# The first projection of a decoder trunk: its loads in halves, products from the first microsecond, small loads later

## The chip, the cores and the metric

One NeuronCore of a Trainium2 chip runs the whole program. The metric is the device time of one execution in microseconds (us); each number below is from one profiled execution or from the three timed runs of the kernel before. The engines are TensorE (PE; its weight loads are PEld), VectorE (DVE), ScalarE (ACT), GpSimd (POOL) and SyncE (SP), which here does nothing but issue DMAs.

## The reference, cut to what matters

One layer: a combined input projection, four token mixers on its columns, gates, an output projection, a LayerNorm, then a mixture of 16 experts and another LayerNorm. x is 256 rows by 1024, float32.

```python
def mixer(x, w_in, ...):
    proj = jnp.einsum("bsd,de->bse", x, w_in)          # 1024 -> 10264 columns
    (a_in, gdn_qkv, ...) = jnp.split(proj, offsets, axis=-1)
    ...
    qkv = jax.nn.silu(causal_depthwise_conv(gdn_qkv, gdn_conv_w))
    ...
    return jnp.einsum("bsd,de->bse", merged, w_out)

def reference(x, ...):
    h = mixer(x, ...)
    x = layer_norm(DN_ALPHA * x + h, ...)
    h = moe(x, ...)
    return layer_norm(DN_ALPHA * x + h, ...)
```

## The kernel before

Every product of the mixer is made in two parts: an operand is split into a rounded high part (`xh`, `whi`, ACT's copy) and the rest (`xl`, `wlo`, DVE's subtraction), and three products (high by high, high by low, low by high) are accumulated in PSUM. `proj_cm` (L277) makes 256 columns of the input projection: two blocks `b` of 128 columns, 8 row blocks `k`, so 2 times 24 products of 128x128 by 256 columns: for a block the 16 with `whi` (L266, L270), then the 8 with `wlo` (L275). Its weights are one 1 MB load (`fetch`, L109) into one of three buffers `raw`; the casts (`parts`, L119) go into `whi` and `wlo`, three buffers each; its result is one of three PSUM tiles `pcm`.

The work before the first product: x comes in four 256 KB loads (L145), left half of both row tiles first; PE transposes it (L258) in four groups of four, and `split` makes `xh` and `xl`. The first weights come as two halves by columns (L146), each with all rows. `one0`, a constant 1 made out of `xh`, scales the first casts, so that these stand behind the splits.

The steps of the mixer are written in a list, `ORDER`, which calls the functions in turn: `bi.0` to `bi.5` (`b_in`) are the six projections of the DeltaNet branch with its convolution, `cq`, `gg`, `lg` and `dq` other projections, `sm` the small one (L374: two loads of 64 and 32 bytes at a time). `bi.0` also calls `taps` (L330): one PE transpose `pp` of the 11 small parameter vectors that L165 loads into `prm_r`. From it come `prm` and `cwh`, the convolution's taps, which every ACT and DVE instruction that empties a `pcm` of `b_in` needs (L401, L404). `consts` (`cc`) makes `aexp` from `hp8` on ACT (L348).

SP's DMAs are issued in the order in which the program names them. The other engines' instructions are ordered beforehand by a planner: of the instructions whose inputs it takes to be there at that point of its own simulated time, the earliest in program order goes next. An engine executes its list in that order and waits in place. `tc.keep_in_program_order` ties an instruction behind the one named before it on its engine. DMAs of SP use eight completion semaphores in turn, so that a DMA is issued when the eighth before it has landed.

After the mixer (16 merge steps), the output projection and the router, the experts' weights stream through a ring of buffers (`ew`, from about 300 us on) while PE multiplies.

Of the kernel before, what the change touches and what calls it, by code (L numbers as in the profile page):

```python
# [18 lines left out]
S = 256  # L19
# [3 lines left out]
E = 16  # L23
# [14 lines left out]
MORDER = (1, 3, 2, 0)  # L38
HELD = (14, 15, 7, 12, 13, 24)
ORDER = """  # L40
bi.0 cc bi.1 bi.2 cq.0 bi.3 sm bi.4 cq.1 bi.5 bs gg.0 bp.0 bv.0 cq.2 bp.1 bo lg.0
dq.0 ba.1 lg.1 bb dq.1 dq.2 dq.3 bx.0 ba.0 dv.0 bx.1 dg bl.0.0 dv.1 bl.1.0 bl.0.1 cv.0 de
bl.2.0 da.0 bl.1.1 da.1 bv.1 cq.3 b0 bl.2.1 rt ds do.1 b1 cw.0 cv.1 do.0 cw.2 cw.1 cy.0
gg.1 ai.0 cy.1 by ai.1 dy al
# [2 lines left out]
C_A, C_GQ, C_GBD, C_GG, C_SQ, C_SV = 0, 512, 2048, 2056, 2568, 3592  # L47
# [4 lines left out]
def trunk(ctx: ExitStack, tc: tile.TileContext, a, out):  # L52
    nc = tc.nc
    V, A, G, T, Q = nc.vector, nc.scalar, nc.gpsimd, nc.tensor, nc.sync

    ctx.enter_context(tc.manual_schedule(engines={mybir.EngineType.SP}))
    cst = ctx.enter_context(tc.tile_pool(name="cst", bufs=1, side="left"))
# [19 lines left out]
    pmm = psm.enter_context(tc.tile_pool(name="pmm", bufs=3, space=PSUM))  # L77
# [5 lines left out]
    def PJ(name, shape=(128, 4, S)):  # L83
        return act.tile(list(shape), F32, name=name, tag="pj", bufs=NPJ)
# [10 lines left out]
    def pb(name, shape=(128, 4, 128)):  # L95
        return pbr.tile(list(shape), F32, name=name, tag="pb")

    def split(ps, hi, lo, scale=None):
        if scale is None:
            A.copy(hi, ps)  # L100
            V.tensor_tensor(lo, ps, hi.bitcast(F32), op=OP.subtract)  # L101
# [7 lines left out]
    def fetch(src, cuts=1):  # L109
# [4 lines left out]
        for c in range(cuts):  # L114
            cs = slice(c * n // cuts, (c + 1) * n // cuts)
            Q.dma_start(raw[:, :, cs], src[:, :, cs])
        return raw

    def parts(raw, k0, nk, c0, n, one=None):  # L119
# [6 lines left out]
        cuts = (slice(0, nk),) if one is None else (slice(0, nk // 2), slice(nk // 2, nk))  # L126
        for c in cuts:
            if one is None:
                A.copy(hi, src)  # L129
            else:  # L130
                A.activation(hi[:, c], src[:, c], AF.Copy, scale=one)  # L131
# [21 lines left out]
    for nm, ap in (("cw_g", a["gdn_conv_w"][0].rearrange("k (b c) -> (k b) c", c=128)),  # L153
# [10 lines left out]
        n = ap.shape[0]  # L164
# [16 lines left out]
    for j, nm in enumerate(("rg_w_a", "rg_w_x")):
        w4 = a[nm][0].rearrange("(b t) i o -> t i b o", t=2)
        for t in range(2):
            G.dma_start(rgw[64 * t:64 * t + 64, j, :, 64 * t:64 * t + 64], w4[t])
    wgu = mk.tile([16, 512], F32, name="wgu")
    G.dma_start(wgu, a["gla_w_gate_up"][0])
    gb1 = cst.tile([128, 2, 8], F32, name="gb1")
    wr = lc.tile([128, 8, E], F32, name="wr")
    G.dma_start(wr, a["w_router"].rearrange("(k p) e -> p k e", p=128))
    rb = cst.tile([128, E], F32, name="rb")  # L190
    G.dma_start(rb, bc_rows(a["router_bias"], E))
    V.tensor_scalar(rb, rb, 0.5, None, op0=OP.add)

    lnr = cst.tile([128, 128], F32, name="lnr")
    G.memset(lnr, 0.0)
    for j, nm in enumerate(("ln1_g", "ln1_b")):
        G.dma_start(lnr[8 * j:8 * j + 8, :], a[nm][0].rearrange("(b c) -> b c", c=128))
# [52 lines left out]

    xh = xtp.tile([128, 8, S], F32R, name="xh")
    xl = xtp.tile([128, 8, S], F32R, name="xl")
    one0 = cst.tile([128, 1], F32, name="one0")
    for kg in range(2):
        for n in range(2):
            p = pb("pxt")
            for k in range(4):
                T.transpose(p[:, k, :], x0[n][:, (4 * kg + k) * 128:(4 * kg + k + 1) * 128], ident)  # L258
            split(p, xh[:, 4 * kg:4 * kg + 4, n * 128:(n + 1) * 128],
                  xl[:, 4 * kg:4 * kg + 4, n * 128:(n + 1) * 128])  # L260
    A.activation(one0, xh[:, 4, 0:1].bitcast(F32), AF.Copy, scale=0.0, bias=1.0)

    def mm3(o, sh, sl, mh, ml, kt, first=True, last=True, wm=False):

# [610 lines left out]
    def merge(i):  # L875
# [32 lines left out]
        cw=c_w, cy=c_y, ai=a_in, al=a_lru, m=merge, cc=consts, rt=router_consts)  # L908
# [493 lines left out]
```

## Time and profile before

| | us |
|---|---|
| median of three timed runs | 634.64 |
| the three runs | 632.44, 634.64, 639.71 |
| the profiled execution's own time | 628.88 |
| its span (first to last instruction) | 627.2 |
| lies around the span | 1.7 |

The span is what the profile shows; its own time adds what lies around it. The timed runs differ among themselves by 7.3 us.

### The profile page before, as it was taken

How to read it: one execution, taken by the hardware profiler on the slowest of the kernel's cores; microseconds unless marked ns; L12 is line 12 of the kernel's file. 1: busy time of each engine (PE TensorE's matmuls, PEld its weight loads, DVE VectorE, ACT ScalarE, POOL GpSimd, SP SyncE). 2: the span in 40 equal slices, each digit the busy share in tenths (PEclk: the TensorE clock that was granted, in tenths of full speed). 3: DMA queues.
4: the chain of work that ended last, by engine and by line, in shares of the span. 5: the costliest groups of instructions: out<-in, count | busy, mean ns of one | idle time of the engine just before them, and what ended most of it. 6: DMA issues, size and time to landing. Idle time of an engine off the chain costs nothing.

```text
span 627.2 us, 10612 instructions
## 1 busy us (share of the span) xinstructions
PE 592.7 (95%) x4217; PEld 464.3 (74%) x4217; DVE 323.4 (52%) x640; ACT 253.6 (40%) x423; POOL 31.1 (5%) x70
## 2 busy tenths in 40 slices
PE   5999999999998899999999999999999999999980
PEld 4999999999998799999999999534443533534250
DVE  3798888666447888555556656551210211200145
ACT  4466654464379586443435445210311211211021
POOL 8000011000002100000000000000000000000002
PEclk9999999998799999999999999999999999999995
DMA  8775454730412325789998796999999999999962
GB/s 221 215 219 185 135 180 124 217 102 2 135 68 85 118 68 165 222 301 320 361 361 303 258 362 231 345 331 389 404 390 387 402 397 386 400 399 386 381 235 72
DMA packets 109955, 160.93 MB, mean 257 GB/s; under 512 B 6566, under 2 KB 57132, under 8 KB 109900
## 3 DMA queue, kind: packets, MB, share of 16 engines
q1 hardware_dynamic: 109420, 159.55, 73.4%
q0 software_dynamic: 480, 0.64, 0.5%
q8 instruction: 35, 0.57, 0.4%
q14 instruction: 20, 0.16, 0.1%
HBM read 159.00 MB, written 1.18 MB: 255 GB/s over the span
## 4 chain that ended last, share of the span: by engine, by line
PE 68%; DMA 5%; DVE 4%; issue 4%; ACT 1%; POOL 1%; SPq 0%; POOLq 0%; DVEq 0%
PE wu L1257 8%; PE wg L1257 8%; PE pd L1266 8%; PE pcm L275 6%; PE pcm L270 5%; PE pcm L266 5%; DMA ew<-in_w_down_dram 3%; PE pbr L266 2%; PE pxg L1180 2%; PE pbr L275 2%; PE pbr L270 2%; DMA ew<-in_w_up_dram 2%; PE pa L739 1%; PE pwo L266 1%; PE pwo L268 1%
## 5 line engine op out<-in xcount | busy, mean ns | idle before, releaser
L133 DVE TENSOR_TENSOR wlo<-raw,whi 128x1024 fp32r<-128x1024 f32 (+1 forms) x106 | 126.7, 1206 | 56.9 <-ACT whi L129 48.1
L129 ACT CAST whi<-raw 128x1024 fp32r<-128x1024 f32 x102 | 105.9, 1047 | 103.6 <-DMA raw<-in_w_in_dram 33.8
L266 PE MATMUL pcm<-xh,whi 128*128 128x256 f32 x512 | 126.2, 284 | 2.4 <-ACT whi L131 2.4
L270 PE MATMUL pcm<-xl,whi 128*128 128x256 f32 x512 | 125.8, 283 | 0.0
L266 PEld LDWEIGHTS pcm<-xh,whi 128*128 128x128 f32 x512 | 97.9, 191 | 3.1 <-ACT whi L131 2.8
L270 PEld LDWEIGHTS pcm<-xl,whi 128*128 128x128 f32 x512 | 97.8, 191 | 0.0
L275 PE MATMUL pcm<-xh,wlo 128*128 128x256 f32 x512 | 72.3, 283 | 0.1
L275 PEld LDWEIGHTS pcm<-xh,wlo 128*128 128x128 f32 x512 | 66.0, 191 | 0.8 <-DVE wlo L133 0.5
L1266 PE MATMUL pd<-ew,sh 128*64 128x512 f32 (+1 forms) x288 | 59.4, 547 | 1.5 <-ACT sh L1314 0.7
L1257 PE MATMUL wu<-ew,xg 128*64 128x512 f32 x256 | 59.4, 595 | 1.0 <-DMA ew<-in_w_up_dram 1.0
L101 DVE TENSOR_TENSOR dd<-pd,dd 128x512 fp32r<-128x512 f32 (+1 forms) x18 | 11.4, 631 | 94.9 <-ACT dd L100 94.9
L1257 PE MATMUL wg<-ew,xg 128*64 128x512 f32 x256 | 56.7, 595 | 0.6 <-issue 0.6
L1266 PEld LDWEIGHTS pd<-ew,sh 128*64 128x64 f32 x288 | 21.7, 137 | 37.1 <-issue 30.6
L1257 PEld LDWEIGHTS wu<-ew,xg 128*64 128x64 f32 x256 | 18.6, 137 | 39.3 <-issue 32.1
L1257 PEld LDWEIGHTS wg<-ew,xg 128*64 128x64 f32 x256 | 18.1, 137 | 33.6 <-issue 33.0
L266 PE MATMUL ptm<-whi,xh 128*128 128x256 f32 x128 | 32.9, 290 | 0.0
L266 PE MATMUL pbr<-yth,whi 128*128 128x256 f32 x128 | 32.3, 286 | 0.0
L268 PE MATMUL ptm<-whi,xl 128*128 128x256 f32 x128 | 32.1, 284 | 0.0
L270 PE MATMUL pbr<-ytl,whi 128*128 128x256 f32 x128 | 32.0, 282 | 0.0
L100 ACT CAST dd<-pd 128x512 fp32r<-128x512 f32 (+1 forms) x18 | 9.7, 539 | 49.5 <-PE pd L1266 49.5
L1295 DVE SCALAR_TENSOR_TENSOR sh<-wu,cw,sh 128x512 f32<-128x512 f32 x8 | 6.0, 751 | 42.3 <-PE wu L1257 42.3
L1187 ACT ACTIVATE xg<-pxg,gb 128x128 f32<-128x128 f32 x32 | 13.3, 456 | 35.2 <-DVE xg L1186 34.2
(419 smaller groups left out, 903.3 us busy)
## 6 DMA issues: line engine op xcount, KB each, us to landing
raw<-in_w_in_dram SPq DMA_DIRECT2D x39, 1024.0 KB, 6.1
ew<-in_w_gate_dram SPq DMA_DIRECT2D x64, 512.0 KB, 10.4
ew<-in_w_up_dram SPq DMA_DIRECT2D x64, 512.0 KB, 10.3
ew<-in_w_down_dram SPq DMA_DIRECT2D x64, 512.0 KB, 10.3
raw<-in_w_branch_dram SPq DMA_DIRECT2D x8, 1024.0 KB, 4.9
raw<-in_w_out_dram SPq DMA_DIRECT2D x4, 1024.0 KB, 15.6
x<-in_x_dram SPq DMA_DIRECT2D x4, 256.0 KB, 5.6
raw<-in_w_in_dram SPq DMA_DIRECT2D x2, 512.0 KB
```

Source lines behind the costliest of these rows:

```text
L100: A.copy(hi, ps)
L101: V.tensor_tensor(lo, ps, hi.bitcast(F32), op=OP.subtract)
L129: A.copy(hi, src)
L133: V.tensor_tensor(lo[:, c], src[:, c], hi[:, c].bitcast(F32), op=OP.subtract)
L266: T.matmul(o, sh(k), mh(k), start=first and k == 0, stop=False)
L268: T.matmul(o, sl(k), mh(k), start=False, stop=False)
L270: T.matmul(o, sh(k), ml(k), start=False, stop=False)
L275: T.matmul(o, sl(k), mh(k), start=False, stop=last and k == kt - 1)
L1180: P(T.matmul(ps[kg][:, k, :], x[:, n, 128 * (2 * kg + k):128 * (2 * kg + k) + 128], oh[n], start=first and n == 0, stop=last and n == 1))
L1187: A.activation(xg[1][:, 2 * kg + k, :], ps[kg][:, k, 128:256], AF.Identity, scale=g_, bias=b_)
L1257: P(T.matmul(p[r, :], xg[pr][:, k, r], W[pr, (nm, e, k // 2)][:, k % 2, :], start=k == 0, stop=k == 7))
L1266: P(T.matmul(p[r, :], hT[:, k, r], W[pr, ("wd", e, c, k // kn)][:, k % kn, :], start=k == 0, stop=k == 3))
```

## The change

- x's left halves, the upper four row blocks of the first weights (all 256 columns), x's right halves, the lower four row blocks: 0.5 MB each, in this order. The next two weight loads (1 MB each, for `bi.1` and `bi.2`) follow, where before one followed.
- `first_proj` takes the place of `proj_cm` in `bi.0`. It works through the rows as they come: 16 products with `whi` of the upper rows, the transposes of x's right half, 8 products with `wlo`; then the same for the lower rows. Casts are in two pieces each. All of its PE, ACT and DVE instructions are kept in program order.
- `warm` adds products of a zero tile (128 by 256, bfloat16) into a PSUM tile that nothing reads: 10 at the start, 4 after each of the two transpose groups of x's left half, 6 ahead of the first real product, 24 in all.
- `hp8` is loaded by SP after the parameter vectors, where POOL loaded it first; nine other small loads go from POOL to SP and to a step `ll` of `ORDER`, after `bp.0`. The addition on `rb` moves into `rt`. `one0` is gone.

```diff
-bi.0 cc bi.1 bi.2 cq.0 bi.3 sm bi.4 cq.1 bi.5 bs gg.0 bp.0 bv.0 cq.2 bp.1 bo lg.0
+bi.0 cc bi.1 bi.2 cq.0 bi.3 sm bi.4 cq.1 bi.5 bs gg.0 bp.0 ll bv.0 cq.2 bp.1 bo lg.0
...
+    K = tc.keep_in_program_order
...
+            keep(A.copy(hi[:, c], src[:, c]))
         for c in cuts:
-            V.tensor_tensor(lo[:, c], src[:, c], hi[:, c].bitcast(F32), op=OP.subtract)
+            keep(V.tensor_tensor(lo[:, c], src[:, c], hi[:, c].bitcast(F32), op=OP.subtract))
...
+    raw0 = []
     for h in range(2):
         for n in range(2):
             Q.dma_start(x0[n][:, 512 * h:512 * h + 512], xin[:, n, 512 * h:512 * h + 512])
-    raw0 = [fetch(w_in[:, :, C_GQ + 256 * j:C_GQ + 256 * j + 256], 2 - j) for j in range(2)]
+        if h == 0:
+            raw0.append(fetch(w_in[:, :, C_GQ:C_GQ + 256], 4))
+        else:
+            Q.dma_start(raw0[0][:, 4:8], w_in[:, 4:8, C_GQ:C_GQ + 256])
+    raw0 += [fetch(w_in[:, :, C_GQ + 256 * j:C_GQ + 256 * j + 256]) for j in (1, 2)]
...
-    G.dma_start(hp8[:, 0:4], bc_rows(a["gdn_a_log"], 4))
-    G.dma_start(hp8[:, 4:8], bc_rows(a["gdn_dt_bias"], 4))
+    Q.dma_start(hp8[:, 0:4], bc_rows(a["gdn_a_log"], 4))
+    Q.dma_start(hp8[:, 4:8], bc_rows(a["gdn_dt_bias"], 4))
...
+    def late_loads():
+
+        Q.dma_start(wgu, a["gla_w_gate_up"][0])
+        for j, nm in enumerate(("rg_w_a", "rg_w_x")):
+            w4 = a[nm][0].rearrange("(b t) i o -> t i b o", t=2)
+            for t in range(2):
+                Q.dma_start(rgw[64 * t:64 * t + 64, j, :, 64 * t:64 * t + 64], w4[t])
+        Q.dma_start(wr, a["w_router"].rearrange("(k p) e -> p k e", p=128))
+        Q.dma_start(rb, bc_rows(a["router_bias"], E))
+        for j, nm in enumerate(("ln1_g", "ln1_b")):
+            Q.dma_start(lnr[8 * j:8 * j + 8, :], a[nm][0].rearrange("(b c) -> b c", c=128))
...
+    wz = cst.tile([128, S], BF16, name="wz")
+    V.memset(wz, 0.0)
+    idle = pb("idle", (128, S))
+
+    def warm(n):
+
+        for _ in range(n):
+            K(T.matmul(idle, wz[:, 0:128], wz, start=True, stop=True))
+
+    def x_part(kg):
+        ps = []
         for n in range(2):
+            ps.append(pb("pxt"))
             for k in range(4):
...
+            if kg == 0:
+                warm(4)
+
+    def first_proj():
+
+        p = pmm.tile([128, 2, S], F32, name="pcm", tag="mm")
+
+        def low(kg, lo):
+            for b in range(2):
+                for k in range(4):
+                    K(T.matmul(p[:, b, :], lo[:, k, 128 * b:128 * b + 128], xh[:, 4 * kg + k, :],
+                               start=False, stop=kg == 1 and b == 1 and k == 3))
+
+        warm(10)
+        x_part(0)
+        hl = []
+        for kg in range(2):
+            hl.append(parts(raw0[0], 4 * kg, 4, 0, 256, True))
+            if kg == 0:
+                warm(6)
+            for k in range(4):
+                for b in range(2):
+                    for x in (xh, xl):
+                        K(T.matmul(p[:, b, :], hl[kg][0][:, k, 128 * b:128 * b + 128], x[:, 4 * kg + k, :],
+                                   start=kg == 0 and k == 0 and b == 0 and x is xh, stop=False))
+            if kg == 0:
+                x_part(1)
+            low(kg, hl[kg][1])
+        return p
...
-        p = proj_cm(C_GQ + 256 * ci, raw0[ci] if ci < 2 else None, one0 if ci == 0 else None)
+        p = first_proj() if ci == 0 else proj_cm(C_GQ + 256 * ci, raw0[ci] if ci < 3 else None)
         if ci == 0:
             taps()
```

## Rows read from the trace of the kernel before

**Rows 1.** The page: busy time of the engines over the span (share, number of instructions), and TensorE's granted clock in 40 slices of 15.7 us.

```profile
PE 592.7 (95%) x4217; PEld 464.3 (74%) x4217; DVE 323.4 (52%) x640; ACT 253.6 (40%) x423; POOL 31.1 (5%) x70
...
PEclk9999999998799999999999999999999999999995
```

**Rows 2.** Busy time by stretch, in us from the span's start: length, then for PE, PEld, DVE, ACT and POOL the busy us (instructions), then granted clock, DMA share and GB/s.

```profile
0.00:11.50 11.50, 4.17 (x16) 3.00 (x16) 2.89 (x7) 4.57 (x9) 9.62 (x26) 1.00 0.84 205
...
11.50:19.50 8.00, 7.90 (x48) 7.70 (x48) 4.14 (x8) 3.93 (x5) 3.07 (x15) 1.00 0.60 155
...
16.00:18.00 2.00, 2.00 (x19) 2.00 (x19) 0.35 (x2) 0.95 (x1) 0.00 (x0) 1.00 0.08 24
...
20.00:28.00 8.00, 8.00 (x70) 8.00 (x69) 5.66 (x17) 3.21 (x7) 0.00 (x0) 1.00 1.07 349
...
20.00:60.00 40.00, 39.95 (x340) 39.67 (x339) 36.55 (x100) 25.25 (x40) 0.00 (x0) 1.00 0.77 232
...
380.00:390.00 10.00, 9.06 (x76) 8.62 (x75) 4.32 (x23) 5.24 (x10) 0.00 (x0) 1.00 0.57 179
```

**Rows 3.** The timeline of the first 20 us (start, duration, engine, line, operation, tiles; in brackets the engine's idle time before and what ended it), PE, its weight loads, ACT and DVE. ACT's rows of L131 and L129 are the casts of weights, x2 two in a row.

```profile
3.56 2.34 PE L258 MATMUL pxt<-ident,x 128*128 128x128 f32 x8 [3.56 <-DMA x<-in_x_dram]
...
7.17 1.97 PE L258 MATMUL pxt<-ident,x 128*128 128x128 f32 x8 [1.27 <-DMA x<-in_x_dram]
...
9.18 0.59 ACT L100 CAST xh<-pxt 128x512 fp32r<-128x512 f32 x1 [0.27 <-PE pxt L258]
...
9.76 0.20 ACT L348 ACTIVATE aexp<-hp 128x4 f32<-128x4 f32 x1
...
9.79 0.69 DVE L101 TENSOR_TENSOR xl<-pxt,xh 128x512 fp32r<-128x512 f32 x1 [0.16 <-ACT xh L100]
...
10.76 1.33 ACT L131 ACTIVATE whi<-raw,one 128x512 fp32r<-128x512 f32 x2 [0.80 <-DMA raw<-in_w_in_dram]
...
11.53 0.58 PE L266 MATMUL pcm<-xh,whi 128*128 128x256 f32 x1 [2.39 <-ACT whi L131]
...
12.12 0.42 PE L266 MATMUL pcm<-xh,whi 128*128 128x256 f32 x1
...
12.34 0.41 PE L270 MATMUL pcm<-xl,whi 128*128 128x256 f32 x1
...
14.21 1.34 ACT L131 ACTIVATE whi<-raw,one 128x512 fp32r<-128x512 f32 x2 [2.12 <-DMA raw<-in_w_in_dram]
...
16.45 0.28 PE L266 MATMUL pcm<-xh,whi 128*128 128x256 f32 x1
...
16.57 0.28 PE L270 MATMUL pcm<-xl,whi 128*128 128x256 f32 x1
...
17.05 2.00 ACT L129 CAST whi<-raw 128x1024 fp32r<-128x1024 f32 x2 [1.50 <-DMA raw<-in_w_in_dram]
...
18.14 1.23 DVE L133 TENSOR_TENSOR wlo<-raw,whi 128x1024 fp32r<-128x1024 f32 x1 [1.78 <-ACT whi L129]
...
18.33 1.10 PE L275 MATMUL pcm<-xh,wlo 128*128 128x256 f32 x8
...
19.51 0.14 PEld L332 LDWEIGHTS pp<-ident,prm_r 128*128 128x128 f32 x1 [0.28 <-DMA prm_r<-in_ln_g_dram]
...
19.60 0.36 PE L266 MATMUL pcm<-xh,whi 128*128 128x256 f32 x1
```

**Rows 4.** SP's queue: start and duration of each issue; a row with a count merges issues in a row, and then the duration is that of the whole.

```profile
0.81 1.82 SPq L145 DMA_DIRECT2D x<-in_x_dram  x4
...
17.05 0.25 SPq L165 DMA_DIRECT2D prm_r<-in_rg_b_x_dram  x1
...
18.02 0.29 SPq L165 DMA_DIRECT2D prm_r<-in_ln_b_dram  x1
...
18.36 2.74 SPq L116 DMA_DIRECT2D raw<-in_w_in_dram  x3
...
21.15 2.80 SPq L374 DMA_DIRECT2D raws<-in_w_in_dram  x1
...
39.82 0.37 SPq L116 DMA_DIRECT2D raw<-in_w_in_dram  x1
...
44.67 0.37 SPq L116 DMA_DIRECT2D raw<-in_w_in_dram  x1
```

**Rows 5.** The timeline around 30 us: ACT's casts for `bi.2` and `cq.0`, DVE's last step in emptying `bi.0`'s PSUM tile, and PE's first product of `cq.0`.

```profile
24.01 2.00 ACT L129 CAST whi<-raw 128x1024 fp32r<-128x1024 f32 x2 [2.11 <-DMA raw<-in_w_in_dram]
...
27.93 1.05 ACT L129 CAST whi<-raw 128x1024 fp32r<-128x1024 f32 x1 [1.55 <-DMA raw<-in_w_in_dram]
...
30.16 0.47 DVE L404 SCALAR_TENSOR_TENSOR gq<-pcm,cwh,gq 128x253 f32<-128x253 f32 x1
...
30.99 0.28 PE L266 MATMUL pcm<-xh,whi 128*128 128x256 f32 x1
```

**Rows 6.** Two instructions of the step `rt`, on DVE: one in the timeline, one in the view of the tile `wr` (count, then duration in ns least/median/largest, then start).

```profile
21.12 0.17 DVE L352 COPY gb<-prm 128x16 f32<-128x16 f32 x1
...
L355 DVE TENSOR_TENSOR bw<-wr,prm x1: 271/271/271, 106.9 to 106.9; 128x128 f32<-128x128 f32 x1
```

**Rows 7.** PE's 32 small products of L739, and the stretch around their end, as in the view of stretches.

```profile
157.74 5.06 PE L739 MATMUL pa<-qe,kx 128*32 128x32 f32 x32
...
159.50:166.30 6.80, 6.80 (x36) 6.41 (x36) 2.23 (x4) 1.92 (x8) 0.64 (x1) 0.51 0.50 155
```

More of the change, by code (lines that the diff above doesn't have):

```diff
@@ L96, in pb, with split @@
         return pbr.tile(list(shape), F32, name=name, tag="pb")
-    def split(ps, hi, lo, scale=None):
+    K = tc.keep_in_program_order
+    def split(ps, hi, lo, scale=None, keep=lambda i: i):
         if scale is None:
-            A.copy(hi, ps)
-            V.tensor_tensor(lo, ps, hi.bitcast(F32), op=OP.subtract)
+            keep(A.copy(hi, ps))
+            keep(V.tensor_tensor(lo, ps, hi.bitcast(F32), op=OP.subtract))
         else:
@@ L107, in trunk, with fetch @@
     w_in = a["w_in"][0].rearrange("(k p) c -> p k c", p=128)
-    def fetch(src, cuts=1):
+    def fetch(src, rows=None):
         k, n = src.shape[1], src.shape[2]
@@ L113, in fetch, with parts @@
         raw = raw.rearrange("p (k c) -> p k c", k=k)
-        for c in range(cuts):
-            cs = slice(c * n // cuts, (c + 1) * n // cuts)
-            Q.dma_start(raw[:, :, cs], src[:, :, cs])
+        r = slice(0, k if rows is None else rows)
+        Q.dma_start(raw[:, r], src[:, r])
         return raw
-    def parts(raw, k0, nk, c0, n, one=None):
+    def parts(raw, k0, nk, c0, n, cut=False):
         hi = wst.tile([128, 1024], F32R, name="whi", tag="whi", bufs=NHI)[:, :nk * n]
@@ L125, in parts @@
         src = raw[:, k0:k0 + nk, c0:c0 + n]
-        cuts = (slice(0, nk),) if one is None else (slice(0, nk // 2), slice(nk // 2, nk))
+        cuts = (slice(0, nk // 2), slice(nk // 2, nk)) if cut else (slice(0, nk),)
+        keep = K if cut else lambda i: i
         for c in cuts:
[L128 to L131, printed above, removed]
+            keep(A.copy(hi[:, c], src[:, c]))
         for c in cuts:
-            V.tensor_tensor(lo[:, c], src[:, c], hi[:, c].bitcast(F32), op=OP.subtract)
+            keep(V.tensor_tensor(lo[:, c], src[:, c], hi[:, c].bitcast(F32), op=OP.subtract))
         return hi, lo
@@ L176, in trunk @@
     hp8 = mk.tile([128, 8], F32, name="hp8")
-    G.dma_start(hp8[:, 0:4], bc_rows(a["gdn_a_log"], 4))
-    G.dma_start(hp8[:, 4:8], bc_rows(a["gdn_dt_bias"], 4))
+    Q.dma_start(hp8[:, 0:4], bc_rows(a["gdn_a_log"], 4))
+    Q.dma_start(hp8[:, 4:8], bc_rows(a["gdn_dt_bias"], 4))
     rgw = mk.tile([128, 2, 4, 128], F32, name="rgw")
     G.memset(rgw, 0.0)
[L181 to L184, printed above, removed]
     wgu = mk.tile([16, 512], F32, name="wgu")
-    G.dma_start(wgu, a["gla_w_gate_up"][0])
     gb1 = cst.tile([128, 2, 8], F32, name="gb1")
     wr = lc.tile([128, 8, E], F32, name="wr")
-    G.dma_start(wr, a["w_router"].rearrange("(k p) e -> p k e", p=128))
     rb = cst.tile([128, E], F32, name="rb")
-    G.dma_start(rb, bc_rows(a["router_bias"], E))
-    V.tensor_scalar(rb, rb, 0.5, None, op0=OP.add)
     lnr = cst.tile([128, 128], F32, name="lnr")
     G.memset(lnr, 0.0)
-    for j, nm in enumerate(("ln1_g", "ln1_b")):
-        G.dma_start(lnr[8 * j:8 * j + 8, :], a[nm][0].rearrange("(b c) -> b c", c=128))
+    def late_loads():
[8 more added lines that the diff above has]
+            Q.dma_start(lnr[8 * j:8 * j + 8, :], a[nm][0].rearrange("(b c) -> b c", c=128))
     ones = mk.tile([128, 128], F32, name="ones")
@@ L252, in trunk @@
     xl = xtp.tile([128, 8, S], F32R, name="xl")
-    one0 = cst.tile([128, 1], F32, name="one0")
-    for kg in range(2):
+    wz = cst.tile([128, S], BF16, name="wz")
[6 more added lines that the diff above has]
+        ps = []
         for n in range(2):
-            p = pb("pxt")
+            ps.append(pb("pxt"))
             for k in range(4):
[L258 to L261, printed above, removed]
+                K(T.transpose(ps[n][:, k, :], x0[n][:, (4 * kg + k) * 128:(4 * kg + k + 1) * 128], ident))
+            split(ps[n], xh[:, 4 * kg:4 * kg + 4, n * 128:(n + 1) * 128],
+                  xl[:, 4 * kg:4 * kg + 4, n * 128:(n + 1) * 128], keep=K)
+            if kg == 0:
[23 more added lines that the diff above has]
+        return p
     def mm3(o, sh, sl, mh, ml, kt, first=True, last=True, wm=False):
@@ L275, in mm3, with proj_cm @@
                 T.matmul(o, sl(k), mh(k), start=False, stop=last and k == kt - 1)
-    def proj_cm(c0, raw=None, one=None):
+    def proj_cm(c0, raw=None):
         if raw is None:
@@ L282, in proj_cm @@
         for b in range(2):
-            hi, lo = parts(raw, 0, 8, 128 * b, 128, one)
+            hi, lo = parts(raw, 0, 8, 128 * b, 128)
             mm3(p[:, b, :], lambda k: hi[:, k, :], lambda k: lo[:, k, :],
@@ L351, in router_consts @@
     def router_consts():
+        V.tensor_scalar(rb, rb, 0.5, None, op0=OP.add)
         V.tensor_copy(gb1.rearrange("p j k -> p (j k)"), pc("ln_g", 0, 16))
@@ L907, in trunk @@
         cq=lambda c: pair_in(("sq", "sk"), C_SQ, c), cv=lambda c: val_in("sv", C_SV, c),
[L908 removed]
+        cw=c_w, cy=c_y, ai=a_in, al=a_lru, m=merge, cc=consts, ll=late_loads, rt=router_consts)
     for st in ORDER.split():
```

## The prediction

> **What bounds the kernel now.** I began with the page: PE is busy for 95% of the span, and its granted clock is full nearly throughout [rows 1]. Whatever keeps PE from working is therefore the first thing to look for, and the view of stretches shows where it is: in the first 11.5 us PE is busy for 4.2, and from then on it hardly stops (7.9 of 8.0, then 39.95 of 40) [rows 2]. The start alone is in question, and the timeline of it [rows 3] is to be read engine by engine. PE waits for x (first transposes at 3.56, the second pair at 7.17), then for the first casts, which wait for the weights: the first real product starts at 11.53. The second cast pair waits 2.12 us more, until 14.21. The products of the second block end at 19.43 (18.33 + 1.10), and `pp` follows at once, held for 0.28 us by the last parameter vector. `bi.1` starts at 19.60. From there on PE is continuous, so what the change is worth is how much earlier `bi.1` starts, less what is given back further on.
>
> There is a second cost in this stretch. [...] The first 24 products take 4.92 us (11.53 to 16.45), the next 24 take 2.98: 1.9 us for the clock.
>
> **The change part by part.** *Loads.* I take the queue as bytes in a row. Before, x (1 MB) is there soon after 7.17, 1.5 MB at 10.76, 2 MB at 14.21, 3 MB at 17.05 [rows 3]; POOL's small loads ran beside these, and once they are gone and runs are long, the core moves 349 GB/s, or 1 MB in 3.0 us [rows 2]. In the new order the first MB is x's left half and the upper weights: 7.2 us, as 1 MB before (bounds 5.8, from the quarter at 3.56 and 349 GB/s on, and 9.1, the end of the second pair's transposes). From there I count 1.6 us for each half MB, the rate of 20 to 28, because POOL's loads leave this stretch: x's right half at 8.8 (7.3 to 10.8), the lower weights at 10.4 (8.8 to 14.2), `bi.1`'s at 13.4 (11.8 to 17.05), `bi.2`'s at 16.4 (14.8 to 20.1, which is 17.05 and another 3.0).
>
> *The chain to the end of `bi.0`.* Half a cast is 0.67 (1.33 for two), so real products start at 7.9. 16 of them at 0.117 (18.33 less 16.45, over 16) take 1.9: 9.8. Four transposes take 0.5 at the higher level (half of 1.97 is 1.0 for four at the start's pace): both groups by 10.8. Two ACT copies of 0.59 from 10.3, the last subtraction of 0.69: 12.2. The lower casts follow on ACT at 11.5, the lower weights being there since 10.4, and are no later. 16 products: 14.1; the last 8: 15.0. The eight with `wlo` of the upper rows fit in the wait for the splits. `bi.1`'s cast needs 1.0 after 13.4, so it is ready at 14.4. Against 19.60 `bi.1` starts 4.5 us earlier. By the lower bounds of the loads this is 5.9, by the upper ones (lower weights at 14.21, end at 17.8) 1.8.
>
> *Idle products.* The first ten end before x comes: 10 at 0.22 from about 1.2 us (an estimate: SP's first issue at 0.81 [rows 4], and a memset) are over by 3.4. The four behind the first group take 0.9 at the lower level and may hold the second group by 0.4; the ten behind the second group end by 8.1 at that level, about when the first cast is done. They cost at most 0.4, and are meant to buy the 1.9. The trace of before has no such product, so the bounds are 0 and 1.9; I take 1.5 of it as bought, inside the times above. [...]
>
> *What is given back.* `bi.0`'s PSUM tile must be emptied before `cq.0`, the third product group later, may start, and before the change this was close: DVE's last step ended at 30.63, PE began `cq.0` at 30.99 [rows 5]. Emptying needs `cwh`, that is the parameter vectors, and these now lie behind one more MB. Their last four issues come when the eighth DMA before has landed: at 17.05 in the trace, the landing of the third MB, and the transpose could start at 19.51, 2.46 later [rows 3, 4]. In the new order that DMA is `bi.2`'s: 16.4 + 2.46 = 18.9, only 0.6 earlier. What follows was then stretched by waits for loads: the casts of `bi.2` and `cq.0` came at 24.01 and 27.93 after waits of 2.11 and 1.55 [rows 5]. `bi.2`'s weights are now early, and `cq.0`'s load is issued at about 18.3 (vectors' last issue at 17.7, two of `hp8` at 0.3); at the 5.65 us that `bi.2`'s took (18.36 to 24.01) it lands at 23.9. Cast 1.0, subtraction 1.2 [rows 3] and the last step 0.5 give 26.6; PE would be ready at 15.1 + 11.4 (19.60 to 30.99) = 26.5. So `cq.0` starts at about 26.8 instead of 30.99, and 4.5 becomes 4.2; I take 4.0. If the emptying takes as long as it did (19.51 to 30.63), it ends at 30.0 and only 0.6 is left. DVE is busy for 36.6 of 40 us in this stretch [rows 2], but starts earlier as well.
>
> *Late loads.* Nine DMAs enter SP's queue ahead of `cq.2`'s. The nearest row for many small pieces is `sm`'s load, 2.80 us of issue [rows 4]; SP idles from 40.2 to 44.67 between two fetches, and that covers it. If it takes longer, as two of `sm`'s kind in a row might, the fetch is some 2 us late; three buffers put a fetch nearly two groups of 5.7 us ahead of its use: bounds 0 and 2, taken as 0. `rgw`, `wr` and `lnr` are needed much later (`wr` at 106.9 [rows 6]). `one0` and POOL's issues were hidden or are in the 11.5.
>
> **Sum.** 628.88 - 4.0 = 624.9 for the profiled execution, 5.8 below the median. What separates the two lies in every run, so I subtract from the median: 634.64 - 4.0 = 630.6. The shift reaches the end because the experts' stream is not saturated when it begins to matter: DMA share 0.57 at 380 to 390 [rows 2].
>
> **The rivals.** *A: PE waits for the parameter vectors.* `taps` is still called straight after `bi.0`, and in the trace `pp` stands there and waits. If the planner leaves it there, PE stops at 15.0, `pp` starts at 18.9 and `bi.1` at 19.1: 0.5 gained, 634.1. If the lower clock level returns after 4 us of idling, the 1.9 is paid again: 636.0. For it: the order of before. Against it: the planner moves instructions to where it takes the input to have landed. `gb`, of the step `rt`, stands at 21.12 and the next of `rt` at 106.9 [rows 6], and the vectors are now further behind and PE earlier, so that `pp` may well slide into `bi.1`, where a later place costs nothing until 26. [...]
>
> *B (slower): ACT waits for `hp8`.* `aexp` stands ahead of the first casts on ACT (9.76 [rows 3]), since `hp8` was POOL's first load. Now it lands behind the vectors, at about 19.6. If the planner puts `aexp` ahead of `bi.1`'s casts, these end at 20.8 and `bi.1` starts 1.3 late; ahead of the lower casts, 24 products (2.8) follow 19.8 + 0.7, 23.3 against 19.43: 3.9 late. It decides as soon as one cast that PE needs before 19.6 stands behind `aexp`. With 2.5 for the middle: 637.1.
>
> *C: the clock later on.* After the 32 small products at 157.74 the granted clock is 0.51 for 6.8 us [rows 7], and PE loses about 3.4. If another order of instructions spares this, it is 630.6 - 3.4 = 627.2. For it: every later instruction is ordered anew; against: these products stay.
>
> *D: the loads do not come earlier,* and only the order of products changes: the upper bounds above, 1.8 gained, 632.8.
>
> **How the numbers follow.** The forecast has 0.47, A 0.25, B 0.12, C 0.10, D 0.06. The forecast's own range is 628.7 to 634.0 (5.9 and 0.6). For 8 in 10 the range goes from 626.5, inside C, to 637.0, just short of B's middle; outside are half of C, half of B and part of A. This kernel's runs lie 7.3 us apart, so a change under 1% (6.3 us) cannot be told from none. Faster by more needs C, or the best of the loads together with a short emptying: 0.20. Slower by more needs B at its worst and the clock: 0.07. Within: 0.73.
>
> **What would show it.** Right: first real product near 8 us and 0.12 apart from the start; `bi.1` at about 15; `pp` amid `bi.1`'s products; `cq.0`'s first product near 27. Wrong: PE idle from 15 until the vectors land (A); ACT idle ahead of `aexp` (B); no stretch at half clock near 160 (C); the lower weights after 13 us (D). Wrong too if PE, early at 27, waits again for DVE or for raw weights before 60.

## The result and the profile after

| | before | after |
|---|---|---|
| median of 20 runs, us | 632.67 | 636.73 |
| fastest and slowest, us | 627.88, 639.71 | 631.40, 638.44 |
| profiled execution, us (span) | 628.88 (627.2) | 632.46 (630.7) |

The ratio is 1.0065, with a 95% interval from 1.0039 to 1.0091: the changed kernel is slower by 4.1 us. The forecast was 4.0 us less. The time lies inside its range, and the sign is wrong.

The page of after, busy time and granted clock (as [rows 1]):

```profile
PE 597.1 (95%) x4241; PEld 465.1 (74%) x4241; DVE 323.8 (51%) x641; ACT 253.0 (40%) x422; POOL 24.7 (4%) x59
...
PEclk9899999998999999999999999999999999999995
```

PE has more work by 4.4 us, of which the idle products are a part, and the clock has a new dip in the second slice. The timeline of PE at the start shows why (columns as in [rows 3]):

```profile
1.22 2.32 PE L267 MATMUL idle<-wz 128*128 128x256 bf16 x10 [1.22 <-DVE wz L261]
...
8.45 0.39 PE L300 MATMUL pcm<-xh,whi 128*128 128x256 f32 x1 [0.68 <-ACT whi L130]
8.68 0.28 PE L300 MATMUL pcm<-xl,whi 128*128 128x256 f32 x1
8.79 0.28 PE L300 MATMUL pcm<-xh,whi 128*128 128x256 f32 x1
...
14.92 1.10 PE L287 MATMUL pcm<-xh,wlo 128*128 128x256 f32 x8
15.86 0.28 PE L310 MATMUL pcm<-xh,whi 128*128 128x256 f32 x1
...
16.57 0.28 PE L310 MATMUL pcm<-xh,whi 128*128 128x256 f32 x1
19.27 0.30 PE L376 MATMUL pp<-ident,prm_r 128*128 128x128 f32 x1 [2.42 <-DMA prm_r<-in_ln_b_dram]
19.33 0.36 PE L314 MATMUL pcm<-xl,whi 128*128 128x256 f32 x1
...
20.62 1.91 PE L319 MATMUL pcm<-xh,wlo 128*128 128x256 f32 x8
22.33 0.41 PE L310 MATMUL pcm<-xh,whi 128*128 128x256 f32 x1
22.55 0.41 PE L314 MATMUL pcm<-xl,whi 128*128 128x256 f32 x1
...
25.77 0.28 PE L310 MATMUL pcm<-xh,whi 128*128 128x256 f32 x1
...
31.43 0.28 PE L310 MATMUL pcm<-xh,whi 128*128 128x256 f32 x1
```

`bi.0` goes as it should: real products from 8.45, 0.12 apart from the second one on, and `bi.1` begins at 15.86 instead of 19.60, a lead of 3.7 us. Then PE stops. `pp` has indeed slid into `bi.1`, but only behind its first seven products, where it waits 2.42 us for the vectors. About 1 us after PE goes on, the granted clock falls to 0.50 and stays there until 23.7: the products come 0.21 apart (22.33 to 22.55). `bi.2` begins at 25.77, in the kernel before at 25.34. The 48 products of `bi.1` would have ended at 21.5 (15.86 + 48 times 0.118); the stop took 2.6 and the lower clock the remaining 1.6. The lead is gone within 10 us, and `cq.0` begins at 31.43 instead of 30.99 [rows 5].

ACT waits in the same place, for `hp8` (timeline of after, ACT); the second cast of `bi.2` stands behind it:

```profile
16.59 1.05 ACT L130 CAST whi<-raw 128x1024 fp32r<-128x1024 f32 x1 [1.01 <-DMA raw<-in_w_in_dram]
20.35 0.20 ACT L392 ACTIVATE aexp<-hp 128x4 f32<-128x4 f32 x1 [2.71 <-DMA hp<-in_gdn_a_log_dram]
20.86 1.04 ACT L130 CAST whi<-raw 128x1024 fp32r<-128x1024 f32 x1 [0.31 <-DVE cwh L378]
```

The stretches of after (columns as in [rows 2]) show the dip, and the end:

```profile
16.00:20.00 4.00, 1.58 (x14) 1.40 (x13) 2.55 (x3) 1.05 (x1) 0.00 (x0) 1.00 0.10 7
20.00:24.00 4.00, 4.00 (x23) 4.00 (x22) 1.91 (x8) 1.92 (x5) 0.00 (x0) 0.57 0.96 309
...
150.00:160.00 10.00, 10.00 (x76) 9.44 (x75) 5.41 (x16) 3.41 (x8) 0.63 (x1) 0.83 0.01 2
200.00:210.00 10.00, 8.08 (x54) 6.99 (x53) 8.08 (x14) 6.08 (x10) 2.48 (x3) 0.83 0.35 107
430.00:580.00 150.00, 149.67 (x754) 66.05 (x751) 22.99 (x50) 24.16 (x49) 0.00 (x0) 1.00 1.05 386
580.00:610.00 30.00, 26.11 (x116) 10.29 (x113) 6.70 (x13) 4.08 (x7) 0.00 (x0) 1.00 1.01 346
```

The same for the kernel before:

```profile
430.00:580.00 150.00, 150.00 (x762) 66.24 (x760) 23.32 (x51) 24.15 (x49) 0.00 (x0) 1.00 1.05 394
580.00:610.00 30.00, 27.52 (x139) 12.75 (x135) 8.52 (x19) 4.83 (x9) 0.00 (x0) 1.00 0.91 324
```

Between 430 and 580 the DMA engines are fully taken in both (share 1.05), but they move 394 GB/s before and 386 after: 1.2 MB less in these 150 us, or 3 us of loading. Starts of the same instruction in the two traces make the ledger:

| first product of | before | after | after less before |
|---|---|---|---|
| `bi.1` | 19.60 | 15.86 | -3.74 |
| `bi.2` | 25.34 | 25.77 | +0.43 |
| tile `px` | 114.88 | 115.82 | +0.94 |
| branch products `pbr` | 227.64 | 226.57 | -1.07 |
| an expert's `wg` late in the stream | 545.93 | 544.95 | -0.98 |
| last pair's `pd`, third group of 16 | 604.14 | 607.71 | +3.57 |

At 545 the profiled execution of after is 1 us ahead (its stretches at half clock, near 155 and 206, make 6.8 us together, those of before, near 154 and 163 [rows 7], 10.2); in the last 60 us it loses 4.5. There PE has run out of its store of weights and goes at the stream's pace. PE's waits at the end, in after:

```profile
579.32 2.54 PE L1311 MATMUL pd<-ew,sh 128*64 128x512 f32 x8 [0.29 <-DMA ew<-in_w_down_dram]
582.02 2.42 PE L1311 MATMUL pd<-ew,sh 128*64 128x512 f32 x8 [0.15 <-DMA ew<-in_w_down_dram]
```

and the first of them in before:

```profile
585.09 2.43 PE L1257 MATMUL wu<-ew,xg 128*64 128x512 f32 x8 [0.22 <-DMA ew<-in_w_up_dram]
```

### The profile page after: what moved, and what is told of

It reads as the page before. It is cut to its first block, busy times and chain, and to the rows that moved or that the text cites. A ratio compares the mean times of both kernels' runs of the same rounds, so it can differ in the third digit from the quotient of the medians.

```text
span 630.7 us, 10644 instructions
## 1 busy us (share of the span) xinstructions
PE 597.1 (95%) x4241; PEld 465.1 (74%) x4241; DVE 323.8 (51%) x641; ACT 253.0 (40%) x422; POOL 24.7 (4%) x59
## 4 chain that ended last, share of the span: by engine, by line
PE 77%; DMA 10%; DVE 4%; issue 4%; ACT 1%; SPq 1%; POOL 1%; POOLq 0%; DVEq 0%
PE wu L1302 8%; PE wg L1302 8%; PE pcm L319 8%; PE pd L1311 8%; PE pcm L314 8%; PE pcm L310 7%; DMA ew<-in_w_down_dram 3%; PE pxg L1225 2%; PE pbr L310 2%; PE pbr L319 2%; PE pbr L314 2%; DMA raw<-in_w_in_dram 2%; DMA ew<-in_w_up_dram 2%; PE ptm L310 2%; PE ptm L312 2%
## 5 line engine op out<-in xcount | busy, mean ns | idle before, releaser
L130 ACT CAST whi<-raw 128x1024 fp32r<-128x1024 f32 (+1 forms) x106 | 108.3, 1031 | 109.0 <-PE pcm L314 36.1
L314 PE MATMUL pcm<-xl,whi 128*128 128x256 f32 x496 | 121.2, 282 | 0.0
L310 PE MATMUL pcm<-xh,whi 128*128 128x256 f32 x496 | 121.1, 282 | 0.0
L310 PEld LDWEIGHTS pcm<-xh,whi 128*128 128x128 f32 x496 | 94.3, 190 | 0.4 <-issue 0.3
L314 PEld LDWEIGHTS pcm<-xl,whi 128*128 128x128 f32 x496 | 94.3, 190 | 0.0
L319 PE MATMUL pcm<-xh,wlo 128*128 128x256 f32 x496 | 70.1, 283 | 0.7 <-DVE wlo L132 0.5
L319 PEld LDWEIGHTS pcm<-xh,wlo 128*128 128x128 f32 x496 | 63.9, 191 | 1.7 <-DVE wlo L132 1.1
L1311 PE MATMUL pd<-ew,sh 128*64 128x512 f32 (+1 forms) x288 | 62.0, 548 | 3.2 <-DMA ew<-in_w_down_dram 2.3
```

Of the source, the lines that this page charges most:

```text
L130: keep(A.copy(hi[:, c], src[:, c]))
L310: T.matmul(o, sh(k), mh(k), start=first and k == 0, stop=False)
L314: T.matmul(o, sh(k), ml(k), start=False, stop=False)
L1311: P(T.matmul(p[r, :], hT[:, k, r], W[pr, ("wd", e, c, k // kn)][:, k % kn, :], start=k == 0, stop=k == 3))
```

## The experiments: what slowed the experts' stream

Taken by 10 us, the stream of before goes from 450 us on 404, 387, 386, 391, 403, 403, 388, 385 GB/s and so on, with the period of the ring (38 buffers of 4 KB in a partition, about 51 us); that of after stays at 385 to 387. The program's memory layout says what is special about ten of the 38: they are the tiles `y` of the mixer, in the pool `yp`. In before it begins at byte 18688 of each partition, a multiple of 256; the other buffers begin at odd multiples of 32 (139232 and on). The change put `wz` (512 bytes) into the pool ahead of `yp` and took `one0` (32) out: `yp` now begins at 19168, an odd multiple of 32 too. No view of the profile shows an address.

Three theories stood. Theory 1: the start address of a buffer sets the rate at which its 2 KB packets go. Theory 2: the loss is that of the start, the wait for the vectors and the clock. Theory 3: the stream's rate changes with something else, by chance. The first runs:

**The changed kernel with the left addresses of before.** `wz` moves to a pool on the other side of the memory, and 32 idle bytes take the place of `one0`, so that `yp` begins at 18688 again.

```diff
-    wz = cst.tile([128, S], BF16, name="wz")
+    gap = cst.tile([128, 8], F32, name="gap")
+    V.memset(gap, 0.0)
+    wz = mk.tile([128, S], BF16, name="wz")
```

> The changed kernel with the zero tile of the idle products in another pool and 32 bytes of filling where one0 was: every buffer left of the ring in the on-chip memory, the ten y buffers of the experts' ring among them, starts where it did before; order and loads are those of the change. Theory 1 (the address of a ring buffer sets how fast its load is written: 84 or 87 ns for a 2 KB packet): the stretch 440 to 580 us runs at 404 GB/s in parts and 386 in others as before the change, instead of 386 throughout, and the time is 3.3 us under the changed kernel, 633.4. Theory 2 (the loss is the wait for the parameter vectors and the half clock at 20 us): 636.7, as changed. Theory 3 (the rate of the experts' stream differs by chance between executions): 636.7, with rates that bear no relation to the addresses.

Measured: 630.86, ratio to before 1.0001 [0.9969, 1.0033]. The row of the stream is that of before again:

```profile
430.00:580.00 150.00, 150.00 (x762) 66.17 (x760) 23.67 (x51) 24.74 (x50) 0.00 (x0) 1.00 1.05 394
```

**The kernel before with its left pools moved by 32 bytes.**

```diff
     one0 = cst.tile([128, 1], F32, name="one0")
+    gap = cst.tile([128, 8], F32, name="gap")
+    V.memset(gap, 0.0)
```

> The kernel before with nothing but 32 bytes of filling in the first pool, so that the ten y buffers of the experts' ring start at 18720 instead of 18688 bytes, and so on, no longer at multiples of 64. Theory 1: 386 GB/s throughout 440 to 580 us and 3.3 us slower than before, 636.0. Theories 2 and 3: as before, 632.7.

Measured: 635.14, ratio 1.0048 [1.0011, 1.0085], and the stream of after:

```profile
430.00:580.00 150.00, 150.00 (x759) 66.13 (x757) 23.68 (x51) 24.70 (x50) 0.00 (x0) 1.00 1.05 386
```

These two settle the loss: without the shift the changed kernel is as fast as before, within 0.3%, and the shift alone makes the kernel before 3 us slower.

**The ring at a multiple of 64, 128 and 256.** In the kernel before an idle tile of 8, 24 or 56 columns of 4 bytes goes ahead of the ring:

```diff
+    gapr = xac.tile([128, 56], F32, name="gapr")
+    V.memset(gapr, 0.0)
     x_sb = [xac.tile([128, D], F32, name="x_sb", tag="x", bufs=2) for n in range(2)]
```

> The kernel before with 32 bytes of filling on the other side, so that the 28 buffers of the ring which start at odd multiples of 32 bytes start at multiples of 64. Theory 1: 404 GB/s from 440 to 580 us instead of 394 on average, 2.4% of 160 us, 3.8 us faster than before: 628.9. Theories 2 and 3: as before, 632.7.

> The kernel before with 96 idle bytes ahead of the ring: its buffers begin at 139136 bytes, a multiple of 128 but not of 256. If a multiple of 128 is enough, this stream and time are those of the ring at 256 (about 628); if 256 is wanted, the stream keeps 386 to 388 GB/s outside the y buffers and the time is that of before (ratio 0.998 to 1.002). Theory 3: ratio 1.000, too.

> The kernel before with 224 idle bytes a partition ahead of the experts' ring, so that its buffers begin at 139008 bytes, a multiple of 256 (before: 139232). Nothing else moves. Theory 1 (a buffer's start address sets the rate of its 2 KB packets): the 404 to 405 GB/s that only the ten y buffers showed from 430 to 600 us now hold in nearly every 10 us of that stretch but for the buffers at other addresses; about 9 MB are to be moved there, so some 3 to 4 us less at the end: 628 (626.5 to 630), ratio 0.994. Theory 3 (the fast stretches are the work of something else that recurs with the ring): the pattern 404, 404, 386, 386 stays and the time is that of before, ratio 1.000.

> The kernel before with its ring at a multiple of 256 once more, beside the one above on the same chip: 627.5 to 629.5, ratio 0.992 to 0.996. By Theory 1 the stream again holds 404 to 408 GB/s.

(The run that this last one stands beside is that with the vectors ahead of `bi.2`'s weights and `hp8` behind them, the last one below.)

| ring begins at | a multiple of | GB/s, 430 to 580 | median, us | ratio to before |
|---|---|---|---|---|
| 139232 (before) | 32 | 394 | | 1 |
| 139200 | 64 | 395 | 632.37 | 0.9998 [0.9963, 1.0033] |
| 139136 | 128 | 395 | 631.68 | 1.0002 [0.9967, 1.0037] |
| 139008 | 256 | 407 | 628.32 | 0.9931 [0.9903, 0.9960] |
| 139008, a second time | 256 | 407 | 627.75 | 0.9958 [0.9927, 0.9988] |

The row of the ring at 256:

```profile
430.00:580.00 150.00, 150.00 (x762) 66.19 (x760) 23.89 (x52) 24.15 (x49) 0.00 (x0) 1.00 1.05 407
```

64 and 128 bring nothing, which the first expectation had wrong; 256 brings the whole stream to 407 GB/s. Theory 1 stands, with 256 as the only one of the multiples tried here that brings more, and Theory 3 falls. How far past such a boundary a buffer starts makes no difference in these runs: starts 32 (the `y` buffers in the second run), 128, 192 and 224 bytes past it cost the same, 384 to 389 GB/s taken by 10 us, against 402 to 409 for the buffers at a multiple of 256. Of the loads only the address written to differs between these kernels; why a multiple of 256 is faster no run here shows.

## The experiments: where the lead of the start goes

**Vectors ahead of `bi.2`'s weights.** The changed kernel, addresses as changed, with `bi.2`'s load behind the vectors and `hp8`:

```diff
-    raw0 += [fetch(w_in[:, :, C_GQ + 256 * j:C_GQ + 256 * j + 256]) for j in (1, 2)]
+    raw0.append(fetch(w_in[:, :, C_GQ + 256:C_GQ + 512]))
...
     Q.dma_start(hp8[:, 4:8], bc_rows(a["gdn_dt_bias"], 4))
+    raw0.append(fetch(w_in[:, :, C_GQ + 512:C_GQ + 768]))
```

> The changed kernel with the weights of bi.2 loaded behind the parameter vectors and hp8 instead of ahead of them; addresses as changed. Theory 2: the vectors land at about 16.0 instead of 19.2 us, PE does not stop in bi.1 (2.4 us less) and the clock does not fall at 20 us (1.6 less): bi.2 starts at about 21.8 instead of 25.8 and the time is 4 us under the changed kernel, 632.7. Theory 1 alone (the stream's end sets the time whatever the start does): 636.7. Both at once: 632.7, with the stream still at 386 GB/s.

Measured: 633.97, ratio 1.0036 [0.9996, 1.0076], the stream at 386. PE's only wait in this stretch is now for `bi.2`'s cast:

```profile
15.84 0.30 PE L377 MATMUL pp<-ident,prm_r 128*128 128x128 f32 x1
...
23.76 0.39 PE L311 MATMUL pcm<-xh,whi 128*128 128x256 f32 x1 [1.97 <-ACT whi L130]
```

The lead at `bi.2` is 1.6. At `px` (114.73) 0.15 of it is left: the wait for the vectors can be taken out of the start, and the lead does not reach the end. So that the addresses hide nothing, the next kernels all have the left addresses of before and the ring at 256, and are to be held against 628.3.

**Only the addresses.** 

> The changed kernel with the left addresses of before and the ring at a multiple of 256, nothing else: the wait for the vectors and the half clock at 20 us stay. Theory 1: the stream at 404 to 408 GB/s from 430 us on, 3 to 3.8 us less than with the left addresses alone (630.9): 627 to 628, the same as the kernel before with its ring there (628.3), since the start's lead is used up at 25 us. Theory 3: 630 to 632.

Measured: 629.03, ratio 0.9966 [0.9930, 1.0002], stream 407. The change on top of a good layout is worth nothing that can be told.

**The small loads on POOL from the start.** Vectors and `hp8` issued by POOL, `pp` and `aexp` behind `bi.0`:

```diff
-        Q.dma_start(prm_r[nrow:nrow + n, :], ap)
+        G.dma_start(prm_r[nrow:nrow + n, :], ap)
...
-        T.transpose(pp, prm_r, ident)
+        K(T.transpose(pp, prm_r, ident))
...
-        A.activation(aexp, hp8[:, 0:4], AF.Exp)
+        K(A.activation(aexp, hp8[:, 0:4], AF.Exp))
```

> The changed kernel with the left addresses of before, the ring at a multiple of 256, the eleven parameter vectors and the two rows for `hp8` issued by POOL from the start instead of by SP behind the weights, and `pp` and `aexp` held behind `bi.0`. Theory 2 (the start's lead was lost to the wait for the vectors and to the half clock behind it): no wait of PE at `pp`, no fall of the clock at 20 us, `bi.2` starts 2.5 to 3.5 us before that of the kernel before, and of this lead 1.5 us or more is left at 100 us. Theory 1: the stream at 404 GB/s at the end. Both: 624 to 627, ratio 0.988. Theory 1 alone (the start's lead runs out behind 100 us whatever it is): the time of the kernel before with its ring at 256, about 628.

> The same without any of the idle products on PE. The first products then go at half clock, 0.21 instead of 0.12 apart, until the clock rises: if the idle products buy what was forecast, `bi.1` begins 1 to 2 us later than with them, and the end comes 1 to 2 us later, ratio to it 1.002 to 1.003. If the lead at the start doesn't reach the end, both take the same time within 0.1%.

Measured: 628.06, ratio 0.9944 [0.9911, 0.9978]; without idle products 630.13, 0.9977 [0.9950, 1.0005]. `pp` does not wait, but now everything ahead of it is late. ACT waits longer for the first weights:

```profile
9.23 1.14 ACT L130 CAST whi<-raw 128x512 fp32r<-128x512 f32 x2 [2.11 <-DMA raw<-in_w_in_dram]
```

This cast stood at 7.78 in after. The first product is at 9.90, after 2.24 us of idling, the first 16 are 0.21 apart, and `bi.1` begins at 18.78. With the small loads back in the first 9 us the start loses 2.9 us of its lead (15.86 in after), about half of it by the later weights and half by the clock; there the idle products change nothing in the start (`bi.1` at 18.52 without them). The medians of the two differ by 2.1 us, with intervals that overlap, and no row here shows why.

**`pp` behind `bi.1`.** SP's order as changed; `bi.1`'s products, `pp`, then `bi.2`'s are tied in this order, and `aexp` behind `bi.2`'s casts:

```diff
+        if ci == 0:
+            p = first_proj()
+            v.p1 = proj_cm(C_GQ + 256, raw0[1], keep=K)
+            taps()
...
+        K(T.transpose(pp, prm_r, ident))
         V.tensor_copy(prm, pp)
+        v.p2 = proj_cm(C_GQ + 512, raw0[2], keep=K)
+        K(A.activation(aexp, hp8[:, 0:4], AF.Exp))
```

> The changed kernel (SP's order of loads as the change has it) with the left addresses of before, the ring at a multiple of 256, and the products of `bi.1`, then `pp`, then those of `bi.2` in this order on PE; `aexp` stands behind the casts of `bi.2` on ACT. Theory 2 (the lead at the start was lost to the waits for the vectors and `hp8` and to the half clock behind them): no wait of PE at `pp`, no half clock at 20 us, `bi.2` begins near 21.6 instead of 25.3, and if the lead reaches the end the time is that of the kernel before with its ring at 256 (628.3), less 2 to 3.8: 624.5 to 626.5. Rival: the lead is given back at the stall near 100 us, where DVE is full, or on the way to the experts, and the time stays 627.5 to 629.

> The same without the idle products on PE. Forecast of their worth: the first products 0.21 apart instead of 0.12 until the clock rises, `bi.1` 1 to 2 us later, the end at most as much later (ratio to the kernel with them 1.000 to 1.003).

Measured: 631.85, ratio 0.9987 [0.9950, 1.0023]; without idle products 630.66, 0.9984 [0.9944, 1.0023]. Now PE waits for nothing until `bi.2` is done, which begins at 21.70, 3.6 us ahead of before. Then PE's timeline has this:

```profile
32.03 0.55 PE L312 MATMUL pcm<-xh,whi 128*128 128x256 f32 x1 [4.44 <-DVE splq L367]
```

`cq.0` waits 4.4 us until DVE has emptied the PSUM tile of `bi.0`. This could not begin before `pp`, now at 21.67, was through, and began later still: DVE made two `wlo` ahead of `cwh` (24.45), and ACT, which does the first step of the emptying, did it at 26.33, behind two casts for which it had waited 3.77 us. The wait has moved one tile on and grown; half clock came with it (0.50 from 32 to 34), and at `px` (117.98) this kernel is 3.1 us behind before. Of the idle products this pair gives a clean price: the first 16 products take 1.99 us with them (8.61 to 10.60) and 3.40 without (7.48 to 10.88), 1.4 us. In that one execution the weights came 1.1 earlier without them, so `bi.1` differs by 0.3 (16.02 and 16.29), and the times do not differ.

**Vectors, then `bi.2`'s weights, then `hp8`.** `pp` right behind `bi.0`, `aexp` behind `bi.2`'s casts; run beside the kernel before with its ring at 256 (the second run of it above):

```diff
+    raw0.append(fetch(w_in[:, :, C_GQ + 512:C_GQ + 768]))
     hp8 = mk.tile([128, 8], F32, name="hp8")
...
-        T.transpose(pp, prm_r, ident)
+        K(T.transpose(pp, prm_r, ident))
+        v.p1 = proj_cm(C_GQ + 256, raw0[1], K)
         V.tensor_copy(prm, pp)
+        v.p2 = proj_cm(C_GQ + 512, raw0[2], K)
+        K(A.activation(aexp, hp8[:, 0:4], AF.Exp))
```

> The changed kernel with left addresses as before and the ring at a multiple of 256; the eleven parameter vectors stand on SP's queue behind the weights of `bi.1`, then come the weights of `bi.2`, then the two rows for `hp8`; on PE `pp` stands right behind `bi.0`, and on ACT `aexp` behind the casts of `bi.2`. Theory 2: no wait of PE at `pp` (vectors land near 15.8), `bi.2` begins at 22.5 to 23.8 (before 25.34), bound by its own weights. If a lead of the start reaches the end, the kernel before with its ring at 256 less 1 to 2.5: 625.5 to 627.5. Rival, as the waits near 100 us gave back 1.25 of a lead of 1.57 in an earlier run: 0 to 0.7 left at 115 us, and the time within 1 of that kernel's (627.5 to 629).

Measured: 628.06, ratio 0.9935 [0.9901, 0.9969], against 627.75 and 0.9958 [0.9927, 0.9988] of its neighbour. PE's timeline:

```profile
15.99 0.30 PE L381 MATMUL pp<-ident,prm_r 128*128 128x128 f32 x1
16.05 0.36 PE L313 MATMUL pcm<-xh,whi 128*128 128x256 f32 x1
...
29.61 0.36 PE L313 MATMUL pcm<-xh,whi 128*128 128x256 f32 x1 [2.01 <-DVE splq L368]
...
101.82 1.21 PE L322 MATMUL pcm<-xh,wlo 128*128 128x256 f32 x8 [0.95 <-DVE wlo L132]
```

PE waits for nothing until `bi.2` is done, and the lead is lost at two places further on. This execution and that of the first run with the ring at 256 have their half clock at the same places up to 580 us (from 151, 161 and 390 on), so that their starts can be compared directly:

| first product of | before, ring at 256 | this kernel | difference |
|---|---|---|---|
| `bi.1` | 19.33 | 16.05 | -3.28 |
| `bi.2` | 25.07 | 21.79 | -3.28 |
| `cq.0` | 30.72 | 29.61 | -1.11 |
| `px` | 114.49 | 114.56 | +0.07 |
| `pbr` | 229.25 | 229.03 | -0.22 |
| late `wg` | 549.24 | 549.06 | -0.18 |

3.3 us at the start become 1.1 when `cq.0` waits for DVE to empty `bi.0`, and nothing (0.07 late at `px`) near 100 us, where PE, no longer behind DVE, waits for `wlo`. In neither place did it begin with a full DVE. The timelines of ACT and DVE in this kernel, and last the one DVE row of the kernel before with its ring at 256:

```profile
20.12 1.05 ACT L130 CAST whi<-raw 128x1024 fp32r<-128x1024 f32 x1 [4.70 <-DMA raw<-in_w_in_dram]
21.07 0.47 ACT L454 ACTIVATE gq<-pcm,cwh 128x256 f32<-128x256 f32 x1
...
21.20 1.23 DVE L132 TENSOR_TENSOR wlo<-raw,whi 128x1024 fp32r<-128x1024 f32 x1 [3.62 <-ACT whi L130]
...
96.37 0.17 DVE L566 COPY xd<-ed 64x8 f32<-64x8 f32 x1 [3.91 <-DMA ed<-s]
```

```profile
96.27 0.17 DVE L512 COPY xd<-ed 64x8 f32<-64x8 f32 x1 [2.77 <-DMA ed<-s]
```

At 30 us: `cwh` is there at 17.29, but the first step of the emptying (ACT, L454) stands behind the cast of `bi.2`, and ACT waits 4.70 us for that load. DVE is idle for 3.62 us of this time, and then takes until 29.5. At 100 us: DVE is 1.0 us ahead of the other kernel at 91.3, and waits for `ed`, the second of two small DMAs that POOL sends through DRAM. POOL issues it 0.70 earlier (92.25 against 92.95), but DVE starts on it 4.1 us after the issue instead of 3.3, so 0.10 later than in the other kernel. From there on DVE is full (9.97 of the 10 us from 100 to 110 in both) and the next `wlo` stands in its list. In all fifteen traces of this case `px` begins 18.1 to 18.8 us after DVE's first use of `ed`. Why the DMA took longer no run here shows; a 1 MB load of weights was under way beside it in both.

Theory 2 named the first loss only, and the rival's forecast came true (0 to 0.7 left at 115 us, the time of the kernel before with its ring at 256). Where the lead went is read from these traces; no run here puts the emptying ahead of the cast on ACT, or makes the loads of `ed` faster, so what either would bring is not shown.

## Why the prediction was wrong, point by point

Two terms of the sum failed. What is given back was put at 0.5 us, and by `bi.2` it was 4.2, more than the 3.7 that the start had gained; and the memory layout, which the sum has at nothing, cost the 4.1 us that were measured.

- **First product, pace, end of `bi.0`: right.** 8.45 against 7.9; 0.12 apart from the start; the lower casts at 12.04 against 11.5; `bi.1` at 15.86 against 15.1. The half-MB loads came as counted (349 GB/s makes 1.5 us of half a MB, where the prediction has 1.6; nothing hangs on it). The 0.5 for four transposes, half of their time in before and so an estimate, came as well: eight took 1.04 from 10.45.
- **Idle products: right.** 1.4 measured in the one pair of executions where the first product followed them closely, 1.5 taken; in the end time they do not show. That the 1.9 us they were to buy are the clock's was the author's estimate: no view of before shows it, the stretches having 1.00 for both paces [rows 2]. In after the products are 0.21 apart where the granted clock is 0.50 (20.4 to 23.6), and 0.12 apart where it is 1.00 (24 to 31).
- **Where the vectors land: right, and the consequence missed.** 18.9 forecast, 19.2 found. "`pp` may well slide into `bi.1`, where a later place costs nothing until 26": it slid by seven products, so that the wait of rival A came, moved by 0.7 us. A's outcome with the clock, a gain of 0.5 less 1.9 or 1.4 us late, is near what came: `bi.2` is 0.43 late. Half clock came back behind the wait, as A allowed for: 2.42 us of waiting, then 0.57 of the clock from 20 to 24. Of B the wait is there (2.71 us), ahead of a cast that PE did not yet need.
- **"What is given back", 0.5: the first step that failed.** `cq.0` was put at 26.8 and came at 31.43. In after the wait at `pp` took 2.6 us and the lower clock behind it 1.6, which the sum had at nothing. Even with the vectors early `cq.0` came at 29.61. This is near the step's other bound ("If the emptying takes as long as it did (19.51 to 30.63), it ends at 30.0 and only 0.6 is left"), for another reason: the emptying began no sooner, at 21.07, behind a cast that waited for its load. The row of DVE, 36.6 of 40 us busy [rows 2], was read as room on account of an earlier start; the room was there (3.62 us idle), and the order on ACT kept DVE from using it.
- **"The shift reaches the end because the experts' stream is not saturated": the second.** The row was that of 380 to 390 [rows 2], a gap in the stream: the share is 1.00 in the 10 us before it, and 1.05 from 430 on, and at the end PE waits for the stream. What it would have left of a lead is not shown, since no kernel here brought one that far by its start.
- **`wz` was costed as work and not as 480 bytes of layout.** "`one0` and POOL's issues were hidden" is true of the instructions. The move of the buffers is the whole of the measured loss, as far as the runs can tell: 3.0 us in the kernel before, and 1.0065 becomes 1.0001 [0.9969, 1.0033] without it.
- **Late loads: right.** They are issued from 44.74 on, and the lead does not change between 25 and 97 us (+0.43, +0.41).
- **C came in part, D not.** In the profiled execution of after the granted clock is 1.00 from 158 to 168, where before has 0.51 for 6.8 us. Another stretch, of 3.4 us, has come near 206, and 1.7 us of C's 3.4 are left, most of the 2.0 that after gains between `px` and `pbr`. It was luck and not the order: the first run above, with the same order of steps, has 0.72 from 162 to 168. The loads did come earlier.

Open is why half clock returns at other places in other executions (near 126, 154, 163, 206 and 390 in these traces). It moves single executions of one kernel by several us: over the 20 of after, the time falls by 6 us for each 0.01 of mean granted clock.

## What to carry over

Before costing a start, follow it to the next places where PE needs another engine: a lead that only PE gets is lost at the first of them that did not move with it (here an emptying that stood behind a cast waiting for its load, and a small DMA through DRAM that landed no earlier). An engine that is nearly full over 40 us can still be idle where it counts (DVE, 36.6 of 40 us busy in before, waited 3.62 us there in the last kernel above), so read the waits of that stretch and not its share. Look at the last stretch by itself: after was 1 us ahead there and lost 4.5 to a stream 2% slower. And a new tile in front of other pools moves them all: the kernel before becomes faster than both by 224 idle bytes that put its ring at a multiple of 256 (ratio 0.993 and 0.996), while 32 bytes in another place cost it 0.5%.

## What was not expected of the hardware

Loads of 2 KB rows into SBUF ran at 405 to 409 GB/s, taken by 10 us, when all buffers of the ring started at a multiple of 256 bytes in their partitions (430 to 580 us, ring at 256), and at 384 to 389 in the stretches where they started at a multiple of 32, 64 or 128 only, with all DMA engines taken in both cases (share 1.05). PE's granted clock fell to half behind a wait of 2.42 us in after, about 1 us after it had gone on, and behind one of 2.32 in the run with only the addresses changed, at about the time it went on; behind the waits of 1.97 and 2.01 us shown above it did not fall.
